# A hybrid DeltaNet and attention block: decayed keys in zero-padded tiles of 128 rows, and other orders around them

## The chip, the cores and the metric

One core of a Trainium2 chip. The metric is the device time of one execution in microseconds (us); lower is better. The products run on TensorE (PE), sums and differences on VectorE (DVE), copies, scalings and exponentials on ScalarE (ACT), a part of the differences on GpSimd (POOL), and the DMAs are issued by SyncE (SP).

## What is computed

One layer on 1024 positions of 1024 channels, in float32: a norm, an input projection, four heads of gated DeltaNet and eight heads of banded attention on it, a gated mix of both, an output projection, a second norm, an up projection with a causal convolution and a gate, a down projection, and a last norm. Of the reference, the part that the change is about, over 16 chunks of 64 positions:

```python
kd_c = k * jnp.exp(G[..., -1:] - G)[..., None]        # the decayed keys, 64 x 128 a chunk
gl_c = gam[..., -1]

def step(s, xs):
    w_i, uv_i, p_i, qg_i, kd_i, gl_i = xs
    u = uv_i - jnp.einsum('bhid,bhde->bhie', w_i, s)
    o = jnp.einsum('bhid,bhde->bhie', qg_i, s) + jnp.einsum('bhij,bhje->bhie', p_i, u)
    s = gl_i[..., None, None] * s + jnp.einsum('bhid,bhie->bhde', kd_i, u)
    return s, o
```

and the outer frame:

```python
mix = jax.nn.sigmoid(ga) * (oa @ w_branch_a[l]) + jax.nn.sigmoid(gb) * (ob @ w_branch_b[l])
x = x + mix @ w_out[l]
h = rmsnorm(x, norm_ffn_w[l])
u = causal_dwconv(h @ w_up[l], conv_ffn_w[l]) + conv_ffn_b[l]
gate, up = jnp.split(u, 2, axis=-1)
x = x + (jax.nn.silu(gate) * up) @ w_down[l]
```

## The kernel before

The large projections are products of 128x128 with 128x512. Each float32 operand is split into a high part (a cast by ScalarE) and a low part (the difference, by VectorE or GpSimd), and each product is three: high with low, high with high, low with high (BH and BL are the normed input, whi and wlo a weight, psph the result). They take some 0.23 us each on TensorE. The products inside the DeltaNet are float32 as they are; each is two instructions in the trace (x2).

The program's stages on the chip's clock: norm and first projections to about 60 us; four DeltaNet heads to about 475; attention in four pairs of heads to 746; the mix of both branches to 850; output projection and norm to 940; the up stage to 1365; the down stage to 1578; the last norm.

**DeltaNet.** The loop over h runs from -1 to 3. Stage h issues the chain of head h and prepares head h + 1, with fillers between: projections and convolutions of head h + 2, gate halves (`gates`, 24 products each, of which stage h takes `GFILL[h + 1]`), and z. `gdn_prep` transposes the keys on TensorE into PSUM (psk) and makes nKs (a copy) and Kd (scaled by the decay) from there, both on ScalarE. `gdn_prep2` transposes the values, makes the decays by two exponentials (decb, decT) and then scales nKs and Vs, 128x128 at a time. A triangular solve follows. The tables `APP`, `APK` and `QN` say after how many fillers the solve is applied (`gdn_apply`, which opens U) and the queries' norm is taken (`gdn_qnorm`).

`gdn_chain` does 16 chunks, two (e = 0 and 1) to each p. Each chunk: the product psws of WQ (queries and solved keys, 128 rows) with the state S; VectorE adds it to U (64 rows) and puts its other half in O; the product pss of Kd with U over the chunk's 64 rows; VectorE makes the next S from S and pss. After two chunks comes pso.

An order of the instructions is found by a scheduler from priorities; `behind()` issues what follows after a named instruction (the last product, or the last of another kind that was noted in `last`).

**End of attention.** The last attention pair is woven with what is left of `gates`, then come the projections of the branches (oh and ol of the DeltaNet's output, bh and bl of attention's).

**Up stage.** A Strassen-like form with seven products P1 to P7 for a pair of blocks, with sums in PSUM on VectorE between them. At its start (line 1333 on) the last operands are made from the second norm's transposes, and the first pair of blocks is begun. From here on the order on each engine is the order of the code (`V`, `S`, `G`, `Q` and the first product of each group are pinned).

**Down stage.** The same form: `plan` is P1, P5, P6, P3, P7, P2, P4, eleven steps each, of 12 products. `prep_w` makes, two steps at a time, the sums W of weights (VectorE), their high parts (wdh, ScalarE) and low parts (wdl, VectorE), two steps ahead for the sums.

Of the kernel before, what the change touches and what calls it, by code (L numbers as in the profile page):

```python
# [16 lines left out]
P = 128  # L17
# [18 lines left out]
APP = (10, 10, 10, 2)  # L36
APK = (7, 4, 3, None)
QN = (7, 3, 4, 5)
PR0 = 1
GFILL = (4, 4, 5, 5, 4)  # L40
# [6 lines left out]
def hybrid_kernel(ctx: ExitStack, tc: tile.TileContext, a):  # L47
# [176 lines left out]
    def first_rms(e):  # L224
# [3 lines left out]
        for i in range(4):  # L228
            xt = gp.tile([P, D], F32, tag=("Kd", "U")[i % 2], name="xt", bufs=2)
# [38 lines left out]
    wraw, whi, wlo = (gw.tile([P, KT, P], dt, tag=tg, name="wv") for dt, tg in ((F32, "sq"), (F32R, "nKs"), (F32R, "Vs")))  # L268
# [89 lines left out]

    def bc3(ap, n):

        return ap.unsqueeze(2).broadcast_to([P, NT, n])
# [38 lines left out]
    def gdn_prep(c):  # L400
# [13 lines left out]
        Kd = gp.tile([P, NT, P], F32, tag="Kd", name="Kd", bufs=2)  # L414
# [8 lines left out]
        for e in range(2):  # L423
# [6 lines left out]
            for i in range(4):  # L430
                nc.scalar.activation(Kd[:, 4 * e + i, :], pks[e][:, i, :], AF.Copy, scale=eg[:, 2, 4 * e + i, h:h + 1])
            for i in range(4):
                nc.scalar.activation(jk, nKs[:, 4 * e + i, :], AF.Square, accum_out=ssk[:, 4 * e + i:4 * e + i + 1])
        nc.vector.tensor_scalar_add(ssk, ssk, EPS)
# [6 lines left out]
    def gdn_prep2(c):  # L441
# [19 lines left out]
        nc.scalar.activation(decT.rearrange("p n j -> p (n j)"), psd2, AF.Exp)  # L461
# [24 lines left out]
        for p in range(NT):  # L486
            nc.scalar.activation(nKs[:, p, :], nKs[:, p, :], AF.Copy, scale=nks[:, p:p + 1])
            nc.scalar.activation(Vs[:, p, :], Vs[:, p, :], AF.Copy, scale=bv[:, p:p + 1])
# [34 lines left out]
    def gdn_apply(c):  # L523
# [17 lines left out]
        U = gp.tile([P, NT, P], F32, tag="U", name="U", bufs=2)  # L541
# [14 lines left out]
    def gdn_chain(c):  # L556
# [6 lines left out]
        for p in range(NT):  # L563
            for e in range(2):
# [7 lines left out]
                mm(ps2, Kd[r, p, :], U[r, p, :], start=True, stop=True)  # L572
# [22 lines left out]
    def gdn_qnorm(c):  # L595

        sqq = gw.tile([P, NT, P], F32, tag="sq", name="sqq")
        nc.scalar.activation(sqq, c["WQ"][:, :, 64:192], AF.Square)
        psn = psc.tile([P, 8], F32, tag="c", name="psn")
        for p in range(NT):  # L600
            side.append(lambda p=p: mm(psn[:, p:p + 1], sqq[:, p, :], ones, start=True, stop=True))
        c["psn"] = psn
# [741 lines left out]
    prs[1].P2(True)  # L1344
    sub(BL[:, k1, s], b22, BH.bitcast(F32)[:, k1, s])
# [25 lines left out]
    p, r = prs  # L1371
    p.P5()
    p.sum_q()
    p.sum_pa()
    r.sum_pa()
    p.P6()
    p.sum_pc()
# [93 lines left out]
    def prep_w(k):  # L1471

        n = min(2, NS - 2 * k)
        for s in range(2 * k + 2, min(2 * k + 4, NS)):
            w_sum(s)
# [325 lines left out]
```

## Time and profile before

| | us |
|---|---|
| median of 3 runs | 1591.93 (1590.27 to 1592.96) |
| the profiled execution's own time | 1592.53 |
| its span in the trace | 1590.6 |
| TensorE busy | 1542.7 (97%) |
| VectorE busy | 1120.3 (70%) |
| ScalarE busy | 698.0 (44%) |
| GpSimd busy | 595.6 (37%) |

The span goes from the first instruction of the trace to the last; the time is a little longer. Busy time of TensorE is that in which a product is in work, not that in which it runs at its peak: the ends of products are modelled, products overlap, and only the distance from start to start tells what one costs. The granted clock is 1.00 at 2.4 GHz and 0.5 at 1.2 GHz; its mean over the span is 0.994.

### The profile page before, as it was taken

What the parts mean: (1) busy time and instruction counts of PE and PEld (TensorE: products, weight loads), DVE (VectorE), ACT (ScalarE), POOL (GpSimd) and SP (SyncE); (2) the same over time, 40 slices, a digit from 0 to 9 for tenths busy, and PEclk for the clock granted to TensorE, in tenths of its full rate; (3) what the DMA queues carried; (4) which work ended last, traced back from release to release, by engine and by line L of the source; (5) the groups of instructions that cost most, each with busy time, mean ns of one, the idle gap of its engine ahead of it and who ended that gap; (6) DMA issues with size and microseconds to landing.
All of it is one profiled execution on the core that took longest, in us unless ns stands there. A gap on an engine that the chain in (4) does not pass through costs nothing.

```text
span 1590.6 us, 21158 instructions
## 1 busy us (share of the span) xinstructions
PE 1542.7 (97%) x7687; PEld 1255.8 (79%) x7687; DVE 1120.3 (70%) x2150; ACT 698.0 (44%) x1376; POOL 595.6 (37%) x449
## 2 busy tenths in 40 slices
PE   8999999999999999999999999999999999999997
PEld 6777776877777787888887887888888888788885
DVE  6795867948436878875665566777777777787787
ACT  7535334352225655654222244444444444433344
POOL 2422212212131101110220148877777776233353
PEclk9999999999999999999999999999999999999998
DMA  7021121122131101122654222233332332775533
GB/s 294 27 73 59 56 73 38 46 77 68 60 123 48 32 26 44 36 73 81 194 167 139 90 80 86 90 114 111 115 108 100 100 100 74 246 245 172 177 93 139
DMA packets 74504, 162.03 MB, mean 102 GB/s; under 512 B 15648, under 2 KB 16928, under 8 KB 74400
## 3 DMA queue, kind: packets, MB, share of 16 engines
q1 hardware_dynamic: 74400, 160.68, 30.5%
q8 instruction: 60, 0.98, 0.3%
q14 instruction: 44, 0.36, 0.1%
HBM read 120.55 MB, written 40.11 MB: 101 GB/s over the span
## 4 chain that ended last, share of the span: by engine, by line
PE 49%; DVE 3%; DMA 2%; ACT 1%; issue 1%; SPq 0%; POOL 0%; POOLq 0%; DVEq 0%; ACTq 0%
PE psph L52 8%; PE pb L52 7%; PE psd L52 7%; PE psout L52 5%; PE pc L52 5%; PE pa L52 4%; PE pb L1141 4%; PE psd L1493 3%; PE pc L1141 2%; PE pa L1141 2%; DMA araw<-dA 1%; DVE yu L1155 1%; PE pso L52 0%; DMA oaT<-dO 0%; DVE wdl L1155 0%
## 5 line engine op out<-in xcount | busy, mean ns | idle before, releaser
L82 POOL TENSOR_TENSOR wlo<-wraw,whi 128x1024 fp32r<-128x1024 f32 (+1 forms) x57 | 120.2, 2108 | 464.7 <-ACT whi L81 259.5
L52 PE MATMUL psph<-BH,whi 128*128 128x512 f32 x688 | 280.4, 408 | 10.1 <-ACT BH L220 5.2
L52 PE MATMUL psph<-BH,wlo 128*128 128x512 f32 x688 | 275.9, 401 | 1.7 <-POOL wlo L82 1.7
L52 PE MATMUL psph<-BL,whi 128*128 128x512 f32 x688 | 277.4, 403 | 0.0
L52 PEld LDWEIGHTS psph<-BH,whi 128*128 128x128 f32 x688 | 130.8, 190 | 34.8 <-ACT BH L220 5.9
L1155 POOL TENSOR_TENSOR ol<-wraw,oh 128x512 fp32r<-128x512 f32 x110 | 150.6, 1386 | 9.1 <-ACT oh L1155 9.1
L52 PEld LDWEIGHTS psph<-BH,wlo 128*128 128x128 f32 x688 | 130.8, 190 | 26.0 <-POOL wlo L82 2.1
L52 PEld LDWEIGHTS psph<-BL,whi 128*128 128x128 f32 x688 | 130.7, 190 | 23.1 <-DVE BL L221 1.0
L52 PE MATMUL psd<-wdl,ah 128*128 128x512 f32 (+1 forms) x311 | 121.6, 391 | 5.4 <-DVE wdl L1155 5.4
L1155 POOL TENSOR_TENSOR al<-araw,ah 128x1024 fp32r<-128x1024 f32 (+1 forms) x28 | 70.5, 2518 | 143.7 <-ACT ah L1155 143.6
L1155 POOL TENSOR_TENSOR wraw<-wraw 128x512 f32<-128x512 f32 x86 | 119.5, 1389 | 4.9
L1493 PE MATMUL psd<-wdh,al 128*128 128x512 f32 (+1 forms) x311 | 121.1, 390 | 0.0
L52 PE MATMUL psd<-wdh,ah 128*128 128x512 f32 (+1 forms) x311 | 119.8, 389 | 0.0
L1155 ACT CAST oh<-wraw 128x512 fp32r<-128x512 f32 x110 | 67.8, 621 | 102.0 <-POOL wraw L1155 101.9
L1155 DVE TENSOR_TENSOR wdl<-W,wdh 128x512 fp32r<-128x512 f32 x77 | 88.4, 1186 | 30.7 <-ACT wdh L1155 30.7
L1155 ACT CAST ah<-araw 128x1024 fp32r<-128x1024 f32 (+1 forms) x39 | 40.6, 1041 | 115.9 <-issue 48.8
L81 ACT CAST whi<-wraw 128x1024 fp32r<-128x1024 f32 (+2 forms) x61 | 55.4, 908 | 78.9 <-PE psph L52 55.1
L1155 POOL TENSOR_TENSOR gl<-wraw,gh 128x512 fp32r<-128x512 f32 x42 | 55.9, 1332 | 69.6 <-ACT gh L1155 69.6
L52 PEld LDWEIGHTS psd<-wdl,ah 128*128 128x128 f32 x311 | 58.8, 189 | 20.0 <-DVE wdl L1155 7.9
L1141 PE MATMUL pa<-BH,gh 128*128 128x512 f32 x176 | 68.6, 389 | 0.0
L52 PE MATMUL pa<-BH,gl 128*128 128x512 f32 x176 | 68.5, 389 | 0.0
L52 PE MATMUL pa<-BL,gh 128*128 128x512 f32 x176 | 68.5, 389 | 0.0
(342 smaller groups left out, 3826.2 us busy)
## 6 DMA issues: line engine op xcount, KB each, us to landing
wraw<-w_up SPq DMA_DIRECT2D x44, 512.0 KB, 4.9
wraw<-w_tiles SPq DMA_DIRECT2D x42, 512.0 KB, 3.5
araw<-dA SPq DMA_DIRECT2D x77, 256.0 KB, 3.0
dA<-yu SPq DMA_DIRECT2D x33, 512.0 KB, 3.1
W<-w_down SPq DMA_DIRECT2D x44, 256.0 KB, 4.7
xt<-x SPq DMA_DIRECT2D x16, 512.0 KB, 5.0
dG<-gt SPq DMA_DIRECT2D x16, 512.0 KB, 2.8
ta<-dG SPq DMA_DIRECT2D x16, 256.0 KB, 2.7
```

The lines of the kernel that those rows point to most:

```text
L52: last["mm"] = nc.tensor.matmul(*args, **kw).ins
L81: nc.scalar.copy(hi, src)
L82: (eng or nc.gpsimd).tensor_tensor(out=lo, in0=src, in1=hi.bitcast(F32), op=ALU.subtract)
L1141: i = nc.tensor.matmul(ps, wh[:, k], xh[:, k], start=start and k == 0, stop=False, **kw)
L1155: return lambda *args, **kw: tc.keep_in_program_order(f(*args, **kw))
L1493: i = nc.tensor.matmul(ps, al[:, j, ts], wh[:, es], start=False, stop=stop, **kw)
```

## The change

Six things at once.

1. Kd is no tile from a rotating buffer any more, but two permanent tiles `Kds`, one for even and one for odd heads, with 128 rows for each chunk. GpSimd clears both once. `gdn_prep2` fills the 64 rows of each chunk by ScalarE from nKs in SBUF, 16 copies of 64x128 a head, between the scalings of nKs and Vs and behind the exponential decT. The product pss then runs over 128 rows of Kd and U.
2. Buffers: the loads of x share three buffers (they had four), the third weight of the start uses the room of kf, U has one buffer instead of two, sqq that of zs.
3. The addition to ssk goes from VectorE to GpSimd.
4. Tables: the first stage takes 6 gate halves instead of 4, so two fewer remain for the end of attention; `APP`, `APK` and `QN` shift the solve's application and the queries' norm.
5. At the start of the up stage P5, q, P6 and pc of the first pair are written ahead of the last operands.
6. In the down stage the sums W for P4 (W21 - W12, written over W12, which no later product needs) are made during P2's steps, eleven steps sooner.

```diff
--- before.py
+++ after.py
@@ -33,11 +33,11 @@
 C2 = (0, 3, 3, 1)
 C3 = (0, 4, 4, 4)
 OUT = (0, 3, 5, 3, 8)
-APP = (10, 10, 10, 2)
-APK = (7, 4, 3, None)
-QN = (7, 3, 4, 5)
+APP = (11, 10, 10, 2)
+APK = (2, 4, 3, None)
+QN = (7, 5, 7, 5)
 PR0 = 1
-GFILL = (4, 4, 5, 5, 4)
+GFILL = (6, 4, 5, 5, 4)
 PRI = 4000
 AHEAD = 2
 BAND = 640
@@ -226,7 +226,8 @@
         s = slice(e * HN, (e + 1) * HN)
         psr = psa.tile([P, HN], F32, tag="a", name="psrb")
         for i in range(4):
-            xt = gp.tile([P, D], F32, tag=("Kd", "U")[i % 2], name="xt", bufs=2)
+            pool, tag = ((gp, "U"), (gp, "Lr"), (gw, "vf"))[i % 3]
+            xt = pool.tile([P, D], F32, tag=tag, name="xt")
             nc.sync.dma_start(xt, a["x"][(4 * e + i) * P:(4 * e + i + 1) * P, :])
             ssq = sml.tile([P, 1], F32, tag="ssq", name="ssq")
             nc.scalar.activation(xt, xt, AF.Square, accum_out=ssq)
@@ -265,7 +266,7 @@
     nea = prm[:, 61:65]
     nc.scalar.activation(nea, nea, AF.Exp)
     nc.vector.tensor_scalar_mul(nea, nea, -1.0)
-    wraw, whi, wlo = (gw.tile([P, KT, P], dt, tag=tg, name="wv") for dt, tg in ((F32, "sq"), (F32R, "nKs"), (F32R, "Vs")))
+    wraw, whi, wlo = (gw.tile([P, KT, P], dt, tag=tg, name="wv") for dt, tg in ((F32, "kf"), (F32R, "nKs"), (F32R, "Vs")))
     nc.sync.dma_start(wraw, a["w_tiles"][2 * GH])
     split(wraw, whi, wlo, nc.vector)
     ws.append((whi, wlo))
@@ -356,6 +357,12 @@
         nc.gpsimd.memset(t_, 0.0)
         zts.append(t_)
 
+    Kds = []
+    for i in range(2):
+        t_ = gp.tile([P, NT, 2, P], F32, name=f"Kd{i}")
+        nc.gpsimd.memset(t_, 0.0)
+        Kds.append(t_)
+
     def bc3(ap, n):
 
         return ap.unsqueeze(2).broadcast_to([P, NT, n])
@@ -411,7 +418,7 @@
             en.tensor_tensor(out=gl, in0=m_, in1=bc3(glo.bitcast(F32)[:, :, h], CH), op=ALU.mult)
             gms.append((gh.rearrange("p n j -> p (n j)"), gl.rearrange("p n j -> p (n j)")))
         nKs = gw.tile([P, NT, P], F32, tag="nKs", name="nKs")
-        Kd = gp.tile([P, NT, P], F32, tag="Kd", name="Kd", bufs=2)
+        Kd = Kds[h % 2]
         Vs = gw.tile([P, NT, P], F32, tag="Vs", name="Vs")
         ssk = gp.tile([P, NT], F32, tag="ssk", name="ssk", bufs=2)
         rk = gp.tile([P, NT], F32, tag="rk", name="rk", bufs=2)
@@ -428,10 +435,8 @@
             pks.append(psk.rearrange("p (n d) -> p n d", d=P))
             nc.scalar.copy(nKs[:, 4 * e:4 * e + 4, :], pks[e])
             for i in range(4):
-                nc.scalar.activation(Kd[:, 4 * e + i, :], pks[e][:, i, :], AF.Copy, scale=eg[:, 2, 4 * e + i, h:h + 1])
-            for i in range(4):
                 nc.scalar.activation(jk, nKs[:, 4 * e + i, :], AF.Square, accum_out=ssk[:, 4 * e + i:4 * e + i + 1])
-        nc.vector.tensor_scalar_add(ssk, ssk, EPS)
+        nc.gpsimd.tensor_scalar_add(ssk, ssk, EPS)
         rsqrt(rk, ssk)
         nc.gpsimd.tensor_mul(bv, beta[:, :, h], rk)
         nc.gpsimd.tensor_mul(nb, bv, rk)
@@ -458,7 +463,7 @@
         mm(psd2, mgtR, gms[1][0], start=True, stop=False)
         mm(psd2, mgtR, gms[1][1], start=False, stop=True)
         decT = gp.tile([P, NT, CH], F32, tag="decT", name="decT")
-        nc.scalar.activation(decT.rearrange("p n j -> p (n j)"), psd2, AF.Exp)
+        last["exp"] = nc.scalar.activation(decT.rearrange("p n j -> p (n j)"), psd2, AF.Exp).ins
         nc.vector.tensor_tensor(out=decT, in0=decT, in1=m64[1], op=ALU.mult)
 
         psG = psa.tile([P, HN], F32, tag="a", name="psG")
@@ -483,9 +488,14 @@
             for e in range(2):
                 mm(psQ[e * CH:(e + 1) * CH, p * CH:(p + 1) * CH], kf[:, p * P + e * CH:p * P + (e + 1) * CH],
                    WQ[:, p, 64 + e * CH:64 + (e + 1) * CH], start=True, stop=True)
-        for p in range(NT):
-            nc.scalar.activation(nKs[:, p, :], nKs[:, p, :], AF.Copy, scale=nks[:, p:p + 1])
-            nc.scalar.activation(Vs[:, p, :], Vs[:, p, :], AF.Copy, scale=bv[:, p:p + 1])
+        Kd = c["Kd"]
+        with behind("exp"):
+            for p in range(NT):
+                for e in range(2):
+                    r = slice(e * CH, (e + 1) * CH)
+                    nc.scalar.activation(Kd[r, p, e, :], nKs[r, p, :], AF.Copy, scale=eg[r, 2, p, h:h + 1])
+                nc.scalar.activation(nKs[:, p, :], nKs[:, p, :], AF.Copy, scale=nks[:, p:p + 1])
+                nc.scalar.activation(Vs[:, p, :], Vs[:, p, :], AF.Copy, scale=bv[:, p:p + 1])
         pt = ptA[h % 2]
         for e in range(2):
             r = slice(e * CH, (e + 1) * CH)
@@ -538,7 +548,7 @@
             nc.scalar.copy(zt[r0, :, r1], psx2[r0, 0:256].rearrange("p (n j) -> p n j", j=32))
 
         WQ, nKs, Vs = c["WQ"], c["nKs"], c["Vs"]
-        U = gp.tile([P, NT, P], F32, tag="U", name="U", bufs=2)
+        U = gp.tile([P, NT, P], F32, tag="U", name="U")
         for q in range(2):
             n = slice(4 * q, 4 * q + 4)
             psW = psa.tile([P, HN], F32, tag="a", name="psW")
@@ -569,7 +579,7 @@
                 nc.vector.tensor_add(U[r, p, :], ps[r], U[r, p, :])
                 nc.vector.tensor_scalar_mul(O[rx, p, :], ps[rx], eg[rx, 1, p, h:h + 1])
                 ps2 = psc.tile([P, P], F32, tag="c", name="pss")
-                mm(ps2, Kd[r, p, :], U[r, p, :], start=True, stop=True)
+                mm(ps2, Kd[:, p, e, :], U[:, p, :], start=True, stop=True)
                 S2 = gp.tile([P, P], F32, tag="S", name="S", bufs=3)
                 last["dve"] = nc.vector.scalar_tensor_tensor(out=S2, in0=S, scalar=eg[:, 3 + e, p, h:h + 1], in1=ps2,
                                                              op0=ALU.mult, op1=ALU.add).ins
@@ -594,7 +604,7 @@
 
     def gdn_qnorm(c):
 
-        sqq = gw.tile([P, NT, P], F32, tag="sq", name="sqq")
+        sqq = gp.tile([P, NT, P], F32, tag="zs", name="sqq")
         nc.scalar.activation(sqq, c["WQ"][:, :, 64:192], AF.Square)
         psn = psc.tile([P, 8], F32, tag="c", name="psn")
         for p in range(NT):
@@ -1342,6 +1352,11 @@
         next(steps1)
     prs[1].keep(S)
     prs[1].P2(True)
+    p, r = prs
+    p.P5()
+    p.sum_q()
+    p.P6()
+    p.sum_pc()
     sub(BL[:, k1, s], b22, BH.bitcast(F32)[:, k1, s])
     sub(hf[:, k1], hf[:, k1], tf[:, k1])
     vsplit(hf[:, k1], BH[:, k0, s], BL[:, k0, s])
@@ -1368,13 +1383,8 @@
         Q.dma_start(dA[5:7, i].rearrange("s p t -> p s t"), y1.rearrange("p (s t) -> p s t", s=2))
 
     ys = []
-    p, r = prs
-    p.P5()
-    p.sum_q()
     p.sum_pa()
     r.sum_pa()
-    p.P6()
-    p.sum_pc()
     p.gate_a()
     r.P5()
     r.sum_q()
@@ -1472,7 +1482,10 @@
 
         n = min(2, NS - 2 * k)
         for s in range(2 * k + 2, min(2 * k + 4, NS)):
-            w_sum(s)
+            if plan[s // FH][0] == "P2":
+                w_sum(s + FH)
+            elif plan[s // FH][0] != "P4":
+                w_sum(s)
         for s in range(2 * k, 2 * k + n):
             S.copy(whs[s % 5], w_block(s))
         for s in range(2 * k, 2 * k + n):
```

ScalarE's order in the preparation of the first head, behind the exponential decT. Before (nKs and Vs are the keys and values that are scaled):

```order
L461 ACTIVATE decT<-psd_758 128x512
L383 ACTIVATE th<-acc 128x512
L487 ACTIVATE nKs<-nKs,nks 128x128
L488 ACTIVATE Vs<-Vs,bv 128x128
L487 ACTIVATE nKs<-nKs,nks 128x128
L488 ACTIVATE Vs<-Vs,bv 128x128
L487 ACTIVATE nKs<-nKs,nks 128x128
L488 ACTIVATE Vs<-Vs,bv 128x128
```

The change (Kd filled from nKs, in two halves, with the same scalings between):

```order
L466 ACTIVATE decT<-psd_753 128x512
L496 ACTIVATE Kd_291<-nKs,eg 64x128 x2
L498 ACTIVATE Vs<-Vs,bv 128x128
L497 ACTIVATE nKs<-nKs,nks 128x128
L496 ACTIVATE Kd_291<-nKs,eg 64x128 x2
L498 ACTIVATE Vs<-Vs,bv 128x128
L497 ACTIVATE nKs<-nKs,nks 128x128
L496 ACTIVATE Kd_291<-nKs,eg 64x128 x2
```

Behind the exponential stand 32 instructions instead of 16; the copies to Kd from psk have left the place ahead of decb.

TensorE's order behind the last attention products (pso). Before, gate products of the normed input BH, BL:

```order
L52 MATMUL pso<-PTh_4256,V 128x256
L52 MATMUL pso<-PTl_4257,V 128x256
L52 MATMUL psph<-BH,wlo 128x512
L52 MATMUL psph<-BH,whi 128x512
L52 MATMUL psph<-BL,whi 128x512
L52 MATMUL psph<-BH,wlo 128x512
L52 MATMUL psph<-BH,whi 128x512
```

The change, with the branches' products (oh, ol, bh, bl):

```order
L52 MATMUL pso<-PTh_4350,V 128x256
L52 MATMUL pso<-PTl_4351,V 128x256
L52 MATMUL psph<-oh_6520,wlo 128x512
L52 MATMUL psph<-oh_6526,whi 128x512
L52 MATMUL psph<-ol_6527,whi 128x512
L52 MATMUL psph<-oh_6526,wlo 128x512
L52 MATMUL psph<-oh_7209,whi 128x512
L52 MATMUL psph<-bh_7215,whi 128x512
L52 MATMUL psph<-ol_7210,whi 128x512
L52 MATMUL psph<-oh_7209,wlo 128x512
L52 MATMUL psph<-bl_7219,whi 128x512
L52 MATMUL psph<-bh_7215,wlo 128x512
```

The 43 gate products between the last pso and the first product of a branch are gone from here.

VectorE's order at the start of the up stage, before (q and pc are sums of the first pair, XT3l, BL and hf operands, pa sums of both pairs):

```order
L1155 TENSOR_TENSOR XT3l<-tf,XT3h 128x4x128
L1155 TENSOR_TENSOR BL<-pst,BH 128x4x128
L1155 TENSOR_TENSOR hf<-hf,tf 128x512
L1155 TENSOR_TENSOR BL<-hf,BH 128x4x128
L1155 TENSOR_TENSOR q<-pc,p_8611 128x512
L1155 TENSOR_TENSOR pa<-pa,p_8611 128x512
L1155 TENSOR_TENSOR pa<-pa,p_8700 128x512
L1155 TENSOR_TENSOR pc<-pb,q 128x512
```

and with the change:

```order
L1165 TENSOR_TENSOR XT3l<-tf,XT3h 128x4x128
L1165 TENSOR_TENSOR q<-pc,p_8643 128x512
L1165 TENSOR_TENSOR pc<-pb,q 128x512
L1165 TENSOR_TENSOR BL<-pst,BH 128x4x128
L1165 TENSOR_TENSOR hf<-hf,tf 128x512
L1165 TENSOR_TENSOR BL<-hf,BH 128x4x128
L1165 TENSOR_TENSOR pa<-pa,p_8643 128x512
L1165 TENSOR_TENSOR pa<-pa,p_8732 128x512
```

q and pc have moved ahead of three operands and two sums.

## Rows read from the trace of the kernel before

**Rows 1.** The page's first lines: the span, and each engine's busy time, its share of the span and its instructions.

```profile
span 1590.6 us, 21158 instructions
...
PE 1542.7 (97%) x7687; PEld 1255.8 (79%) x7687; DVE 1120.3 (70%) x2150; ACT 698.0 (44%) x1376; POOL 595.6 (37%) x449
```

**Rows 2.** The table of stretches over the whole span, four of them: from and to, length, then busy time and instructions of each engine, TensorE's granted clock as a share of full speed, the DMA engines' mean share and GB/s.

```profile
163.00:182.00 19.00, 18.49 (x87) 13.42 (x86) 17.15 (x42) 4.90 (x11) 2.88 (x4) 1.00 0.17 56
...
252.00:283.00 31.00, 28.56 (x124) 20.57 (x124) 24.39 (x61) 7.32 (x19) 6.61 (x7) 0.94 0.18 56
...
335.00:358.00 23.00, 23.00 (x164) 16.94 (x164) 14.33 (x37) 14.11 (x53) 4.66 (x6) 1.00 0.11 30
358.00:382.00 24.00, 22.00 (x96) 15.59 (x96) 19.64 (x62) 5.07 (x14) 4.77 (x2) 0.93 0.21 67
```

**Rows 3.** The view of the tile Kd: operation, number, duration in ns (least, median, greatest), first and last start, shapes. The first is the product pss, the second the filling of Kd.

```profile
L52 PE MATMUL pss<-U,Kd x128: 272/373/579, 137.4 to 452.1; 64*128 64x128 f32 x128
L431 ACT ACTIVATE Kd<-psk,eg x32: 359/387/425, 66.8 to 338.4; 128x128 f32<-128x128 f32 x32
```

**Rows 4.** TensorE's timeline from 242.1 to 244.8: start, duration of one (of all together where x2), line, operation, tiles and shapes.

```profile
242.19 0.39 PE L52 MATMUL psph<-BH,whi 128*128 128x512 f32 x1
242.42 0.38 PE L52 MATMUL psws<-S,WQ 128*128 128x128 f32 x2
242.56 0.48 PE L52 MATMUL psph<-BL,whi 128*128 128x512 f32 x1
242.88 0.40 PE L52 MATMUL psph<-BH,wlo 128*128 128x512 f32 x1
243.11 0.40 PE L52 MATMUL psph<-BH,whi 128*128 128x512 f32 x1
243.44 0.48 PE L52 MATMUL pss<-U,Kd 64*128 64x128 f32 x2
243.85 0.50 PE L52 MATMUL psph<-BL,whi 128*128 128x512 f32 x1
244.19 0.39 PE L52 MATMUL psph<-BH,wlo 128*128 128x512 f32 x1
...
244.66 0.39 PE L52 MATMUL psws<-S,WQ 128*128 128x128 f32 x2
```

**Rows 5.** VectorE's timeline of the same stretch; in brackets the time that the engine stood idle ahead of an instruction, and what ended it.

```profile
242.37 0.16 DVE L434 TENSOR_SCALAR ssk<-ssk 128x8 f32<-128x8 f32 x1
242.84 0.28 DVE L569 TENSOR_TENSOR U<-psws,U 64x128 f32<-64x128 f32 x1 [0.32 <-PE psws L52]
...
243.96 0.35 DVE L574 SCALAR_TENSOR_TENSOR S<-S,eg,pss 128x128 f32<-128x128 f32 x1 [0.44 <-PE pss L52]
```

**Rows 6.** VectorE's and TensorE's timelines about 172.5: U and the pss behind it.

```profile
172.43 0.27 DVE L569 TENSOR_TENSOR U<-psws,U 64x128 f32<-64x128 f32 x1
...
172.76 0.49 PE L52 MATMUL pss<-U,Kd 64*128 64x128 f32 x2 [0.51 <-DVE U L569]
```

**Rows 7.** The table of stretches for the instructions on tile Kd alone (x is their number).

```profile
163.00:182.00 19.00, 3.40 (x14) 2.06 (x14) 0.00 (x0) 1.00 0.17 56
...
252.00:283.00 31.00, 4.61 (x19) 2.75 (x18) 0.00 (x0) 0.94 0.18 56
...
358.00:382.00 24.00, 4.19 (x16) 2.56 (x16) 0.00 (x0) 0.93 0.21 67
```

**Rows 8.** The view of line 487, the scaling of nKs on ScalarE: number, duration in ns (least, median, greatest), first and last start.

```profile
L487 ACT ACTIVATE nKs<-nKs,nks x32: 386/391/407, 76.9 to 349.1; 128x128 f32<-128x128 f32 x32
```

**Rows 9.** The start of the up stage: VectorE's timeline (q and pc), TensorE's, and one stretch behind them in the table of stretches.

```profile
959.74 0.68 DVE L1155 TENSOR_TENSOR q<-pc,p 128x512 f32<-128x512 f32 x1
...
961.53 0.68 DVE L1155 TENSOR_TENSOR pc<-pb,q 128x512 f32<-128x512 f32 x1
...
962.27 0.50 PE L1141 MATMUL pb<-XT3h,oh 128*128 128x512 f32 x1 [2.11 <-DVE pc L1155]
...
963.70:967.10 3.40, 3.40 (x9) 2.67 (x9) 1.07 (x2) 0.00 (x0) 3.40 (x3) 0.51 0.85 287
```

**Rows 10.** The end of attention: the timelines of TensorE (the first product behind the last attention product), ScalarE (bh) and VectorE (bl).

```profile
746.77 0.40 PE L52 MATMUL psph<-BH,wlo 128*128 128x512 f32 x1
...
747.36 3.91 ACT L81 CAST bh<-obT 128x1024 fp32r<-128x1024 f32 x4
...
748.52 3.50 DVE L82 TENSOR_TENSOR bl<-obT,bh 128x1024 fp32r<-128x1024 f32 x3 [0.72 <-ACT bh L81]
```

**Rows 11.** The end of the down stage: what TensorE waits for from 1535 to 1575 (total us, times, longest), VectorE's W ahead of wdl, GpSimd's al, the stretch behind them, and VectorE's wdl in P2's steps.

```profile
PE psd L52 <- DVE wdl L1155: 3.9, 3, 2.5
...
1563.37 3.48 DVE L1155 TENSOR_TENSOR W<-W,W 128x512 f32<-128x512 f32 x2
...
1562.74 2.96 POOL L1155 TENSOR_TENSOR al<-araw,ah 128x1024 fp32r<-128x1024 f32 x1
...
1567.90:1571.30 3.40, 3.40 (x10) 2.66 (x9) 2.96 (x5) 2.08 (x3) 1.52 (x1) 0.50 0.34 139
...
1526.21 3.07 DVE L1155 TENSOR_TENSOR wdl<-W,wdh 128x512 fp32r<-128x512 f32 x2 [0.61 <-ACT wdh L1155]
```

**Rows 12.** The start: ScalarE's cast of the tile wv, and the products with it in the view of that tile.

```profile
19.78 1.05 ACT L81 CAST wv<-wv 128x1024 fp32r<-128x1024 f32 x1
...
L52 PE MATMUL psph<-BH,wv x32: 388/389/393, 24.4 to 51.1; 128*128 128x512 f32 x32
```

## The prediction

> **What bounds the kernel now.** I read the page's head first. TensorE is busy for 1542.7 of 1590.6 us (97%); VectorE, ScalarE and GpSimd stand at 70, 44 and 37% [rows 1]. So time comes from two places only: what TensorE's own products take, and the some 48 us in which it waits. The table of stretches then says where the change lands. The four chains of the DeltaNet lie in stretches where TensorE is busy nearly throughout, but with two kinds of cover: in three of them VectorE is busy for 17.15 of 19, 24.39 of 31 and 19.64 of 24 us, elsewhere for less (14.33 of 23) [rows 2]. A busy TensorE is not one at its peak, so I looked at the products one by one. That is where the main term is.
>
> The profiled execution took 1592.53 us (span 1590.6); the sum is made against it. The median shown is 1591.93, 0.6 less, which comes off at the end. A measurement of this kernel can tell about 0.2% (3.2 us) from no change.
>
> **A. The product with the decayed keys.** Every chunk has two fp32 products of 128x128, two instructions each: WQ with S (psws, all 128 rows) and Kd with U (pss, 64 rows now, 128 after the change with half of them zeros). There are 128 pss instructions, 64 pairs [rows 3]. The timeline of TensorE shows both kinds among the same filler products [rows 4]:
> - psws: 242.19 (filler), 242.42 (the pair), 242.56, 242.88: 0.69 us from the start of the filler before to the second one behind.
> - pss: 243.11, 243.44, 243.85, 244.19: 1.08 us.
>
> The difference is 0.39 us a pair. It is no wait for data: U ends at 242.84 + 0.28 = 243.12 and pss starts at 243.44, 0.32 later [rows 4, 5], while at a place where pss did wait for U (172.43 + 0.27 = 172.70) it started at 172.76, 0.06 after it [rows 6]. So the 0.1 us ahead of the pair, the 0.27 inside and the 0.02 behind belong to the 64 rows. With 128 rows I expect the spacing of psws: 64 x 0.39 = 25.0 us is the most that can come back.
>
> Not all will, since a faster TensorE meets the loop S, psws, U, pss, S. After U (243.12) pss would still start some 0.2 later: covered. S starts at 243.96 and ends at 244.31 [rows 5], and the next psws starts at 244.66 [rows 4], 0.30 after the 0.05 that a result needs; TensorE would take 0.29 out of this distance. So a quiet pair keeps all its gain with about nothing to spare, and a pair behind a long VectorE instruction doesn't. The three VectorE-heavy stretches hold 14 + 19 + 16 pss instructions [rows 7], 24 pairs; I let them keep half: 40 x 0.39 + 24 x 0.195 = **-20.3 us**. Bounds: nothing in the 24 pairs, -15.6; everything, -25.0.
>
> **The new fill of Kd.** 8 ScalarE copies of 128x128 from PSUM a head, 0.39 us each [rows 3], become 16 of 64x128 behind the exponential. As each costs between nothing and 0.39, ScalarE gets 0 to 3.2 us more a head. ScalarE is busy 44% [rows 1] and what follows (nKs, Vs scaled, nKs at 0.39 each [rows 8]) feeds the solve of the next head, which fillers cover: **0**, bounds -2 to +2 (gone are copies that hold a PSUM buffer, added are 16 instructions ahead of the solve). If the cover were gone it would be 4 x 3.2 = 13. The two clears and the ssk addition go to GpSimd (37%) with the same answer.
>
> **B. The start of the up stage.** TensorE waits 2.11 us at 962.27 for VectorE's pc, which stands at 961.53 behind q (959.74) and two pa sums [rows 9]; and 1.4 us later the granted clock is 0.51 for 3.4 us [rows 9], that is 1.2 instead of 2.4 GHz, behind the wait in which TensorE stood still. Half of 3.4 is lost: 1.7. With the change q and pc stand ahead of three operand instructions and the pa sums. pc then needs P6 alone, which lies well ahead of P7's end. What is late next are those operands, needed only by later products. Taken **-3.5**; bounds 0 (another instruction becomes as late) and -3.8.
>
> **C. The end of attention.** Two gate halves move forward to the first stage. Before, 43 gate products followed the last attention product (from 746.77 on [rows 10]; 43 x 0.23, the spacing of fillers from 242.19 to 242.42 [rows 4], is 9.9 us), and under them ScalarE split ob (bh, 4 in 3.91 us from 747.36) and VectorE made bl (3 in 3.50 from 748.52) [rows 10]. That cover goes: in the new order five oh products are followed by bh and bl, 19 products with the last of them. Unhindered they are through at 746.77 + 19 x 0.23 = 751.1. But VectorE has ol and four bl, 1.14 apart, from about 748.5: the last ends at 748.52 + 4 x 1.14 + 1.2 = 754.3, TensorE's half column at about 754.8. **+3.7**; bounds 0 and +5.4 (with one stretch at 1.2 GHz, 1.7 as in B). The products themselves are only moved: the first stage gets 48 and gives them back here.
>
> **D. The end of the down stage.** Between 1535 and 1575 TensorE waits 3.9 us in three stalls for wdl, the longest 2.5 [rows 11]. There VectorE makes W (2 in 3.48 us, slowed beside al on GpSimd, 2.96 from 1562.74) ahead of wdl [rows 11]; the clock is 0.50 for 3.4 us behind it, another 1.7 [rows 11]. The change makes these W sums during P2's steps. Two W of 0.68 or so leave each step: 1.36 of the 2.5, and most of the smaller two, up to all 3.9 and the 1.7: -5.6. In P2's steps the sums stand ahead of wdl (1526.21, 3.07 for two, with 0.61 idle ahead [rows 11]); 1.36 more than fills that idle time, so up to +1.5 there, +1 if nothing else is gained. Taken **-3.0**, bounds -5.6 to +1.
>
> **E. Start.** The x loads get three buffers instead of four: the fourth waits for ScalarE's square of the first. The loads are bound by the queue, and the first product with wv comes at 24.4, after its cast at 19.78 [rows 12]. About 1 us of play: **0**, bounds 0 to +1.5.
>
> **Sum.** -20.3 - 3.5 + 3.7 - 3.0 + 0 = -23.1; 1592.53 - 23.1 = 1569.4, as a median 1568.8: **1569**.
>
> **The rivals.**
> 1. VectorE's loop decides in every pair (R2). For: the play after S is about nothing, and short strays such as the 0.16 us ssk instruction ahead of U [rows 5] stand between its links. Against: in the quiet stretches VectorE idles before both U and S [rows 5]. If the 24 heavy pairs keep nothing and the 40 others 0.39 - 0.16 = 0.23, A is -9.2 and the sum -12: **1580**.
> 2. Loads decide inside the pair (R3). If the pair's own time (0.41, 243.44 to 243.85 [rows 4]) comes from loading each matrix only after the product before, the 128 rows keep it and only 0.12 comes back: 40 x 0.12 + 24 x 0.06 = 6.2, sum -9.0: **1583**. Against it: the 128-row psws pair takes 0.14 (242.42 to 242.56 [rows 4]). The Trainium skill ("TensorE: Matmul & The Clock Gate", Part 3, "The mechanism") has it that a weight load overlaps products in flight only where the row group differs; by that a 64-row load would be the better placed one and a padded one would gain nothing inside the pair. The rows of psws, which has all row groups and is spaced closest, disagree.
> 3. The 0.39 has nothing to do with the rows (R4): U as a freshly written operand, say. Then A is 0 and the sum -2.8: about **1589**. Against: U was ready 0.32 before.
> 4. Slower (R5): ScalarE's burst of 32 instructions behind the exponential (32 x 0.29 = 9.4 us, the mean of 0.39 and half of it for the 64-row ones) stands in front of the U copies that open the next head's chain. With no cover at all this is 4 x 9.4 = 37.6 against a gain of 23.1: **about 1606**. It decides from 6 us a head on. Against: 16 such instructions stand there now, and in the stretch with the last of them (last start of nKs 349.1 [rows 8]) TensorE is busy for all of its 23 us [rows 2].
>
> **How the numbers follow.** Chances: forecast 0.66, R2 0.18, R3 0.05, R4 0.06, R5 0.05. The forecast's own range is 1559 to 1578 (A between its bounds, B, C and D not all at one end). To hold 8 in 10 the whole reaches up to R2 and R3: 1559 to 1583; R4 and R5 are left out with the outer tails. Only R5 is slower: 0.05; R4 stands at the limit of 0.2%, half of its chance is no change: 0.03; the rest is faster: 0.92.
>
> **What would show it.** A right: 128-row pss pairs with the spacing of psws (about 0.14 to the next product), and TensorE's waits for U and S in the heavy stretches no more than doubled. Wrong: spacing of 0.41 kept, or a wait for U or S at most pairs. B: no wait for pc, no half clock behind 963. C: a new wait for bl near 750. D: less wait for wdl from 1540 on, and perhaps some from 1512. The burst: waits of TensorE for ScalarE's U, nKs or WQ copies near the start of each chain; these would make the whole prediction wrong.

## Result, and the profile after

The changed kernel takes 1572.84 us (median, 1570.79 to 1573.51), the kernel before 1592.33 beside it: ratio 0.9878, 95% interval [0.9861, 0.9895], 19.5 us less. A second measurement later gave 0.9894 [0.9879, 0.9908]. The forecast was 1569 in a range of 1559 to 1583, 23.1 us less. The profiled execution took 1573.51, with a span of 1571.7. The head of its page answers to [rows 1]:

```profile
span 1571.7 us, 21185 instructions
...
PE 1520.5 (97%) x7687; PEld 1246.0 (79%) x7687; DVE 1122.3 (71%) x2146; ACT 715.4 (46%) x1408; POOL 597.3 (38%) x455
```

TensorE's busy time fell by 22.2 us at the same number of instructions (7687). The starts of landmark products on TensorE, in us, show where the time went (the last column is the change within the stage that ends there):

| landmark | before | after | shift | in the stage |
|---|---|---|---|---|
| first product with wv | 24.45 | 25.65 | +1.20 | +1.2 |
| last product of attention | 746.65 | 737.59 | -9.06 | -10.3 |
| last product with oh, near the end of the branches | 841.38 | 824.71 | -16.67 | -7.6 |
| first product of the up stage | 939.43 | 922.73 | -16.70 | 0.0 |
| first product of the down stage | 1361.14 | 1340.99 | -20.15 | -3.4 |
| last instruction | 1590.59 | 1571.72 | -18.87 | +1.3 |

48 products of 0.227 us more lie ahead of attention's end now (43 of the gates and 5 with oh): 10.9 us of work moved out of the stage of the third row into that of the second. So the heads and attention became 21.2 us shorter, the end of attention 3.3 longer, the up stage 3.4 shorter, and the down stage 1.3 longer where 3.0 less had been forecast.

**The pairs.** TensorE's timeline of a pss and a psws among fillers answers to [rows 4], and VectorE's U and S beside it to [rows 5]:

```profile
246.75 0.40 PE L52 MATMUL psph<-BH,whi 128*128 128x512 f32 x1
246.99 0.38 PE L52 MATMUL pss<-U,Kd 128*128 128x128 f32 x2
247.12 0.48 PE L52 MATMUL psph<-BL,whi 128*128 128x512 f32 x1
247.44 0.39 PE L52 MATMUL psph<-BH,wlo 128*128 128x512 f32 x1
247.67 0.40 PE L52 MATMUL psph<-BH,whi 128*128 128x512 f32 x1
247.90 0.40 PE L52 MATMUL psws<-S,WQ 128*128 128x128 f32 x2
248.05 0.48 PE L52 MATMUL psph<-BL,whi 128*128 128x512 f32 x1
...
246.49 0.28 DVE L579 TENSOR_TENSOR U<-psws,U 64x128 f32<-64x128 f32 x1 [0.38 <-PE psws L52]
...
247.41 0.35 DVE L584 SCALAR_TENSOR_TENSOR S<-S,eg,pss 128x128 f32<-128x128 f32 x1 [0.25 <-PE pss L52]
```

From the filler ahead of pss (246.75) to the second product behind (247.44) it is 0.69 us, where it was 1.08. pss starts 0.22 after U has ended (246.77), as worked out. S ends at 247.76 and psws follows at 247.90, 0.14 later, where it was 0.35.

Why the rows matter is seen in the weight loads (TensorE's loads, PEld, after and then before):

```profile
246.82 0.36 PEld L52 LDWEIGHTS pss<-U,Kd 128*128 128x128 f32 x2
247.10 0.19 PEld L52 LDWEIGHTS psph<-BL,whi 128*128 128x128 f32 x1
...
243.44 0.29 PEld L52 LDWEIGHTS pss<-U,Kd 64*128 64x128 f32 x2 [0.37 <-DVE U L569]
243.85 0.19 PEld L52 LDWEIGHTS psph<-BL,whi 128*128 128x128 f32 x1
```

After, Kd's load starts at 246.82 and its product at 246.99; the load of the filler behind starts at 247.10, ahead of its product at 247.12. Before, Kd's load and its product both stood at 243.44, and the next load stood at 243.85 with its product [rows 4]: neither the 64-row load nor the 128-row load behind it was made ahead of time. Over all 64 pairs the first load of Kd starts 0.15 us ahead of its product (median), where it was 0.00. So by these rows the 0.39 us are loads that did not lie behind a running product; why a 64-row load is not made ahead, no run shows. The Trainium skill ("TensorE: Matmul & The Clock Gate", Part 3, "The mechanism") says that a load overlaps products in flight only where the row group differs. These rows are against it: loads of all 128 rows overlap products of all 128 rows, and the load of 64 of them didn't. The same section of the Trainium skill also lets a load be pulled ahead into a background weight buffer. Loads of 128 rows do start ahead here, but no row shows which buffer a load goes to.

The loads also show where the reserve behind S went. The load for psws, after and then before:

```profile
247.81 0.30 PEld L52 LDWEIGHTS psws<-S,WQ 128*128 128x128 f32 x2 [0.18 <-DVE S L584]
...
244.43 0.42 PEld L52 LDWEIGHTS psws<-S,WQ 128*128 128x128 f32 x2
```

What it loads is WQ, the operand that the kernel names first, not S, and still it starts 0.05 us after S has ended (247.76). It does so in 55 of the 64 pairs, before in 7; the load of Kd starts 0.05 after U's end in 59, before in 6. The reserve is used up. The products lose little by it: the median psws pair takes 0.02 us more.

The view of the tile Kd, as in [rows 3]:

```profile
L52 PE MATMUL pss<-U,Kd x128: 270/274/378, 140.9 to 443.2; 128*128 128x128 f32 x128
L496 ACT ACTIVATE Kd<-nKs,eg x64: 384/394/400, 73.1 to 353.1; 64x128 f32<-64x128 f32 x64
```

A copy of 64 rows costs ScalarE as much as one of 128, 0.39 us: the fill took the upper bound, 3.2 us more a head, and nobody waited for it.

**What TensorE waits for.** From 60 to 240, then at the end of attention (736 to 850), then in P2 and P4 (1496 to 1563):

```profile
PE psph L52 <- DVE gt L171: 3.1, 3, 1.8
PE psdec L52 <- issue: 1.4, 1, 1.4
PE psph L52 <- DVE u L381: 1.0, 1, 1.0
PE pss L52 <- DVE U L579: 0.9, 1, 0.9
...
PE psph L52 <- DVE bl L82: 0.9, 4, 0.4
PE psph L52 <- ACT oh L81: 0.6, 1, 0.6
...
PE psph L52 <- ACT bh L81: 0.4, 1, 0.4
...
PE psd L52 <- DVE wdl L1165: 3.4, 3, 1.7
PE psd L52 <- ACT wdh L1165: 1.5, 1, 1.5
```

The wait for pc at the start of the up stage is gone, those for bl, bh and oh are new, and the waits of the down stage are 4.9 us in all where they were 3.9 [rows 11].

### The profile page after: what moved, and what is told of

Same layout as the page of the kernel before. It is cut to its first block, busy times and chain, and to the rows that moved or that the text cites. A ratio compares the mean times of both kernels' runs of the same rounds, so it can differ in the third digit from the quotient of the medians.

```text
span 1571.7 us, 21185 instructions
## 1 busy us (share of the span) xinstructions
PE 1520.5 (97%) x7687; PEld 1246.0 (79%) x7687; DVE 1122.3 (71%) x2146; ACT 715.4 (46%) x1408; POOL 597.3 (38%) x455
## 4 chain that ended last, share of the span: by engine, by line
PE 49%; DVE 3%; issue 2%; DMA 1%; ACT 1%; SPq 1%; POOL 0%; POOLq 0%; DVEq 0%; ACTq 0%
PE psph L52 8%; PE pb L52 7%; PE psd L52 6%; PE psout L52 5%; PE pa L52 5%; PE pc L52 5%; PE pb L1151 4%; PE psd L1506 3%; PE pa L1151 2%; PE pc L1151 2%; DVE wdl L1165 1%; DVE yu L1165 1%; PE pso L52 1%; SPq L1165 1%; DMA araw<-dA 1%
## 5 line engine op out<-in xcount | busy, mean ns | idle before, releaser
L52 PEld LDWEIGHTS psd<-wdh,ah 128*128 128x128 f32 x311 | 58.8, 189 | 14.1 <-ACT wdh L1165 1.9
```

Of the source, the lines that this page charges most:

```text
L52: last["mm"] = nc.tensor.matmul(*args, **kw).ins
```

## The experiments

Ratios are to the kernel before, measured beside them; the changed kernel stands at 0.9878 and, measured again, 0.9894. A sum over the pairs is the time from the start of the product before a pair to that of the second behind it, over all 64 pairs, waits included. A stage's length is from its first product to the next stage's, that of P4 to its 133rd product (its last step comes in halves).

### Only the rows undone

```diff
-                mm(ps2, Kd[:, p, e, :], U[:, p, :], start=True, stop=True)
+                mm(ps2, Kd[r, p, e, :], U[r, p, :], start=True, stop=True)
```

> The changed kernel, but the product pss runs over the chunk's 64 rows again (the padded tiles, their fill and all other parts of the change stay). Theory (the rows set the distance of the products around pss): in the changed kernel's trace the 64 pss pairs with the product before and the two behind sum to 49.8 us, before to 69.9, while the psws pairs grew from 46.1 to 49.3; both go back, so 16.9 us are lost and the time is about 1572.8 + 16.9 = 1589.7, with 0.41 us from pss to the next product instead of 0.14. Up to 3.4 more if the two stretches at 1.2 GHz come back that the chains had before. Rival (the gain is due to the new order, the new fill or the buffers and not to the rows): 1573, whatever pss's distances.

Measured: 1587.93 us, ratio 0.9987 [0.9978, 0.9996]. The pss pairs sum to 68.7 us (49.8 in the changed kernel), the psws pairs to 45.5 (49.3): 15.1 us together. Its timeline has the old distance, 0.42 from pss to the next product, with the new tiles, fill and order all there:

```profile
249.42 0.40 PE L52 MATMUL psph<-BL,whi 128*128 128x512 f32 x1
249.74 0.48 PE L52 MATMUL pss<-U,Kd 64*128 64x128 f32 x2
250.16 0.49 PE L52 MATMUL pso<-U,ptA 128*128 128x128 f32 x2
```

This one line is worth 14.8 to 17.3 us (0.9987 less 0.9894 or 0.9878, of 1590): the rows carry nearly nine tenths of the gain (16.9 to 19.4).

### The padded keys alone

The kernel before with the tiles `Kds`, their fill and product, the buffers, ssk and QN; the other tables, the up stage and the sums as before:

```diff
-APP = (11, 10, 10, 2)
-APK = (2, 4, 3, None)
-GFILL = (6, 4, 5, 5, 4)
+APP = (10, 10, 10, 2)
+APK = (7, 4, 3, None)
+GFILL = (4, 4, 5, 5, 4)
-            if plan[s // FH][0] == "P2":
-                w_sum(s + FH)
-            elif plan[s // FH][0] != "P4":
-                w_sum(s)
+            w_sum(s)
...
```

> The kernel before with the padded tiles alone (their fill behind the exponential, the product over 128 rows, the buffers, ssk on GpSimd and the table QN, which the buffers need); gate halves, the solve's table, the up stage and the down stage's sums as before. Theory: 16.9 us come back in the pairs, 1.2 are lost at the start to the third buffer of x, and 0 to 3.4 come from stretches at 1.2 GHz that don't occur: 1592.3 - 16.9 + 1.2 = 1576.6, down to 1573. Rival (the two gate halves, moved to the first stage, are what makes the heads faster, as cover for waits): 1590 or more.

Measured: 1578.77, ratio 0.9930 [0.9915, 0.9945], 11.1 us below the kernel before, which is between the theory and its rival. The pairs give 13.1 us (pss 52.0 for 69.9, psws 51.0 for 46.1), and four stretches at 1.2 GHz lie ahead of 200 us (near 62, 76, 151 and 188). Waits stand there that the first profile of the changed kernel doesn't have, or has shorter (60 to 240 us):

```profile
PE pss L52 <- DVE U L579: 3.2, 2, 1.9
PE psd L52 <- DVE gil L418: 1.8, 1, 1.8
PE psoT L644 <- ACT O L636: 1.5, 1, 1.5
...
PE psB L52 <- DMA zt<-dZ: 0.8, 1, 0.8
```

To the changed kernel it is 5.7 to 8.3 us (0.9930 less 0.9894 or 0.9878, of 1590). The two profiles are 5.6 us apart. From the first product with wv to the first of the up stage this one is 6.8 us longer, and in the up stage 1.8; the start is 1.6 and the down stage 1.5 shorter. The 6.8 are the most that the tables can have here. The next run finds 1.8 of them in the gate halves. But the wait for gil and the stretches near 62 and 76 belong to the execution: the profile of "al on VectorE" below has them too, and there each engine's order in the heads is that of the changed kernel, and heads and attention take 2.9 us longer than in its first profile. What of the rest is the earlier solve (`APK`) and what the other two stretches at 1.2 GHz (1.7 each) stays open.

In the up stage this profile has the old wait of 2.1 us for pc (until 950.82), but no half clock behind it:

```profile
951.00:957.00 6.00, 6.00 (x27) 4.96 (x28) 3.96 (x6) 2.81 (x5) 5.76 (x5) 1.00 0.63 186
```

### The gate halves back

```diff
-APP = (11, 10, 10, 2)
+APP = (10, 10, 10, 2)
-GFILL = (6, 4, 5, 5, 4)
+GFILL = (4, 4, 5, 5, 4)
```

> The changed kernel with the two gate halves back at the end of attention (and the first stage's solve applied one filler sooner, as the shorter list of fillers needs). The prediction's step C (moving them gave nothing ahead of the attention and cost 3.7 behind it): about 3.5 us faster than the changed kernel. Rival, from the runs so far (padded keys alone came to 0.993 of before and the whole change to 0.988, 8 us more, of which the up stage is 3.5 and the down stage -1.3): the halves cover waits in the first stage, and these come back with up to three stretches at 1.2 GHz of 1.7 each: 4 to 6 us slower than the changed kernel. Then the wait for bl after the attention is gone and waits for gil, U or O ahead of 190 us are there.

Measured: 1574.77, ratio 0.9906 [0.9889, 0.9922], against 1572.96 for the changed kernel measured beside it: 1.8 slower, with intervals that overlap, so less than the rival expected and not the gain of step C. The trace shows both sides. From the last attention product to the last with oh it is 94.3 us (before 94.7; the changed kernel 87.1 and the 10.9 moved, 98.0): no wait for bl, 3.7 us better. But in the first stage (60 to 240), and the stretch behind it:

```profile
PE psB L52 <- DMA zt<-dZ: 2.8, 1, 2.8
...
131.00:137.80 6.80, 6.80 (x60) 5.63 (x57) 0.00 (x0) 1.09 (x3) 0.00 (x0) 0.50 0.23 80
```

The solve's trip through DRAM has no cover any more, TensorE waits 2.8 us for it (until 129.22), and the clock of 0.50 for 6.8 us behind costs 3.4. The moved halves cover a wait here and uncover one there.

### The changed kernel once more

> The changed kernel as it is, beside the next three on the same chip. 0.9878 of the kernel before, as first measured; its profile shows in which places the granted clock falls to 0.5 from one execution to the next.

Measured: 1572.96, 0.9894. The first product with wv came at 24.65 (25.65 in the first profile, 24.09 to 27.12 in the other runs with three buffers): the start differs from execution to execution by more than the 1.2 us in the table above. The clock fell near 1555 (1556 in the first profile) and at the very end, and nowhere in the heads.

### The start of the up stage undone

```diff
-    p, r = prs
-    p.P5()
-    p.sum_q()
-    p.P6()
-    p.sum_pc()
     sub(BL[:, k1, s], b22, BH.bitcast(F32)[:, k1, s])
...
     ys = []
+    p, r = prs
+    p.P5()
+    p.sum_q()
     p.sum_pa()
     r.sum_pa()
+    p.P6()
+    p.sum_pc()
```

> The changed kernel with the start of the up stage in its old order. Theory B: the wait of 2.1 us for pc comes back, and with it the stretch at 1.2 GHz (1.7): 1572.8 + 3.5 = 1576.3. Rival (the 3.5 us came from a stretch at 1.2 GHz that the shifted stages before would have avoided anyway): 1572.8 + 0 to 2, with the wait but with the granted clock at 1.00.

Measured: 1575.84, ratio 0.9910 [0.9896, 0.9923], 2.5 to 5.1 us slower than the changed kernel. The up stage takes 421.7 us, as before, against 418.3. The wait is back, and so is the half clock behind it (944 to 950 at 0.72, 1.7 us lost), although everything ahead of it had shifted by 17 us:

```profile
PE pb L1151 <- DVE pc L1165: 2.1, 1, 2.1
...
944.00:950.00 6.00, 5.12 (x15) 4.09 (x16) 3.29 (x6) 1.47 (x3) 5.76 (x5) 0.72 0.56 175
```

The wait comes with the order, in each of the three profiles that have it. The half clock doesn't always: with the padded keys alone it was absent, and the up stage took 420.1.

### The sums back

```diff
-            if plan[s // FH][0] == "P2":
-                w_sum(s + FH)
-            elif plan[s // FH][0] != "P4":
-                w_sum(s)
+            w_sum(s)
```

> The changed kernel with the sums W for P4 made two steps ahead, as before. The prediction's step D (the sums stood in the way of wdl at the end): 1572.8 + 3.0 = 1575.8. The rival that the two traces suggest (P2's steps lost 0.9 us and P4's 0.5 by the move, and the stall at the end belongs to GpSimd's al, beside which any VectorE instruction takes 2.9 us): 1572.8 - 1.3 = 1571.5, with P2 in 31.1 us and P4 in 34.1 instead of 32.0 and 34.6.

Measured: 1571.61, ratio 0.9884 [0.9871, 0.9898]: the times don't tell it from the changed kernel, but the stages do. P2 takes 31.1 us (32.0 in the changed kernel) and P4 34.15 (34.6), as forecast by the rival. Moving the sums cost 1.4 us; it saved nothing.

### al on VectorE

```diff
-        (V if k % 2 and plan[2 * k // FH][0] in ("P5", "P6", "P7", "P4") else G).tensor_tensor(
+        (V if plan[2 * k // FH][0] == "P4" or k % 2 and plan[2 * k // FH][0] in ("P5", "P6", "P7") else G).tensor_tensor(
```

> The changed kernel with every al of P4 made by VectorE, where now every other one is GpSimd's. Theory (the stall at the end of the down stage comes from GpSimd's al, beside which the VectorE instruction that starts then, W before and wdl now, takes 2.9 us instead of 0.7): the wait for wdl of 0.86 goes, al itself costs VectorE 1.2, P4 becomes 0.9 us shorter or more; the 1.5 us wait for the last ah stays, since that waits for a DMA. Rival (VectorE is simply full there): P4 gets longer by the 1.2 us of each added al, 2 to 3 us in all.

Measured: 1568.81, ratio 0.9867 [0.9853, 0.9882], 4.2 below the changed kernel measured beside it. P4 takes 29.7 us instead of 34.7. First VectorE and GpSimd in the changed kernel, then VectorE at the same place of this one:

```profile
1541.56 1.29 DVE L1165 SCALAR_TENSOR_TENSOR ot<-x,rsf,wn 128x1024 f32<-128x1024 f32 x1 [0.38 <-POOL rsf L1165]
1542.77 3.48 DVE L1165 TENSOR_TENSOR wdl<-W,wdh 128x512 fp32r<-128x512 f32 x2
...
1542.13 2.96 POOL L1165 TENSOR_TENSOR al<-araw,ah 128x1024 fp32r<-128x1024 f32 x1
...
1541.48 1.28 DVE L1165 SCALAR_TENSOR_TENSOR ot<-x,rsf,wn 128x1024 f32<-128x1024 f32 x1 [0.38 <-POOL rsf L1165]
1542.68 1.22 DVE L1165 TENSOR_TENSOR al<-araw,ah 128x1024 fp32r<-128x1024 f32 x1
1543.81 1.29 DVE L1165 TENSOR_TENSOR wdl<-W,wdh 128x512 fp32r<-128x512 f32 x2
```

Two wdl take 3.48 us beside GpSimd's al, just as the two W did at this place before [rows 11], and 1.29 without it. With al of 1.22 on its own queue VectorE is through at 1545.1 instead of 1546.25. The expectation was too small (0.9) and held the 1.5 us wait for the last ah to stay: it fell to 0.4, and the half clock behind it (1.7 us) is gone too.

### al on VectorE, sums back, operand loads ahead of the output's

```diff
+            w_sum(s)
...
+        (V if plan[2 * k // FH][0] == "P4" or k % 2 and plan[2 * k // FH][0] in ("P5", "P6", "P7") else G).tensor_tensor(
...
-        if k > 2 and 2 * (k + 2) < NS:
-            a_load(k + 2)
         while loads and loads[0][0] <= s + 1:
...
         if s + 4 == NS - 1:
             prep(k + 2)
+        if 2 * (k + 3) < NS:
+            a_load(k + 3)
```

> The changed kernel with the sums W for P4 made two steps ahead as before, every al of P4 on VectorE, and each load of the down stage's operand issued ahead of the output's DMAs that wait for the norm, instead of behind them. Theory: P2 takes 31.1 us instead of 32.0; in P4 the wait behind GpSimd's al and the 1.5 us for the last ah go, 34.6 becomes 31.5 to 32.5 (29.9 is a stage with no wait, 1.7 less where no stretch at 1.2 GHz follows a wait): 3 to 4 us faster than the changed kernel. Rival (the sums are too much for VectorE beside al): P4 stays above 34.

Measured: 1568.82, ratio 0.9868 [0.9853, 0.9882]. P2 31.1 and P4 31.3, beside 32.0 and 29.7 in the run before: the sums put back give 0.9 in P2 and cost 1.6 in P4 once al is on VectorE. So if the earlier loads do nothing, the move of the sums pays 0.7 there, which the times don't show; of the loads themselves no gain is seen.

### al of P2 as well

```diff
-        (V if k % 2 and plan[2 * k // FH][0] in ("P5", "P6", "P7", "P4") else G).tensor_tensor(
+        (V if plan[2 * k // FH][0] in ("P2", "P4") or k % 2 and plan[2 * k // FH][0] in ("P5", "P6", "P7") else G).tensor_tensor(
```

> The changed kernel with every al of P2 and of P4 on VectorE (the sums W for P4 stay in P2's steps). Theory (the stalls for wdl in both stages come from GpSimd's al, beside which a VectorE instruction takes up to 2.9 us): P2 from 32.0 to about 30.5, P4 29.7 as in the run with P4's al alone, the whole 1.5 us below that run: 0.986 of the kernel before. Rival (P2's VectorE is full: evacuations, the sums W, wdl and now al): P2 stays at 32 or grows, the whole as in that run (0.9867) or slower.

Measured: 1566.72, ratio 0.9847 [0.9832, 0.9862], the fastest version: 24 us below the kernel before and 5 to 7.5 below the changed one. P2 takes 30.3 us and P4 29.5. Of the waits for wdl nothing is left between 1494 and 1562:

```profile
PE psd L52 <- ACT wdh L1165: 0.2, 1, 0.2
```

### O on ScalarE

```diff
-                nc.vector.tensor_scalar_mul(O[rx, p, :], ps[rx], eg[rx, 1, p, h:h + 1])
+                nc.scalar.activation(O[rx, p, :], ps[rx], AF.Copy, scale=eg[rx, 1, p, h:h + 1])
```

> The changed kernel with the other half of psws, O, scaled by ScalarE instead of VectorE (64 instructions of 0.36 us less in VectorE's queue, between U and S of each chunk). Theory (what the 128 rows save, 20.1 us in the pss pairs, is partly given back because the loop of U and S on VectorE now comes just in time: psws pairs 49.3 us instead of 46.1, TensorE's waits for U and S 9.2 instead of 5.9): the psws pairs fall towards 46 and the waits for U and S to 6 or less, the heads become 3 to 6 us shorter. Rival (the loop isn't limited by VectorE's queue but by its own latency, S to psws to U to pss to S): waits for U and S stay at about 9, no change within 1 us, or slower where ScalarE's queue delays O ahead of pso's addition.

Measured: 1579.11, ratio 0.9927 [0.9913, 0.9941], slower than the changed kernel. The waits up to 480 us:

```profile
...
PE pss L52 <- DVE U L579: 3.7, 3, 1.6
PE psws L52 <- DVE S L584: 3.1, 3, 1.7
PE pss L52 <- ACT O L580: 3.0, 2, 1.8
...
PE psB L52 <- DMA zt<-dZ: 1.5, 1, 1.5
```

U and S cost 6.8 us instead of 9.2, but pss waits 3.0 for O, and the psws pairs grow from 49.3 to 50.8 us. Two stretches at 1.2 GHz (near 258 and 357, 1.7 each) lie in the heads; heads and attention take 3.7 us longer than in the first profile of the changed kernel. So the loop is not freed by taking this work off VectorE. The scheduler's order changed with it (a wait for zt appears), so whether latency alone sets the loop stays open.

## Why the prediction was right, and where it was wrong

**A, the rows: the mechanism right, the size too large.** The distance fell from 1.08 to 0.69 in quiet pairs as worked out, and undoing that line alone takes 14.8 to 17.3 us back. The pss pairs gave 20.1 of the possible 25.0 us. What was underrated is the other product: a quiet pair was to keep "all its gain with about nothing to spare", yet the psws pairs grew by 3.2 us (0.685 to 0.707 in the median quiet pair, the rest as waits for S). TensorE's idle time for U in the heads grew from 4.5 to 7.3 us, that for S from 1.4 to 1.9; these lie in the pairs' sums, as do waits too short to show as idle. So -16.9 in the trace (-13.1 with the old tables), instead of -20.3. R2 had the loop decide in every pair. The loads do wait for S and U in nearly every pair, but the products follow 0.05 us behind S in 15 pairs only (3 before) and behind U in 10 (6 before), so R2's price was not paid.

**What filled the gap** had no term. In the heads before, TensorE waited 0.9 us for Kd, 1.7 for wlo and 0.7 for gih, and two stretches at 1.2 GHz cost 1.7 each; in the changed kernel's profiles none of these is there. The half clock is not even in the same place for one order of instructions. Seven profiles have the changed kernel's order in the heads, on every engine: both of its own, and those of the runs with the sums back, the up stage undone, and al on VectorE (three). Two stretches at 1.2 GHz lie ahead of 475 us in two of them (near 55 and 116, and near 62 and 76), one in a third (57), none in the other four; heads and attention are 18.2 to 21.7 us shorter than before. So what of the 3.4 us belongs to the change stays open.

**The fill: right.** Twice as many instructions at 0.39 us, the upper bound of 3.2 us a head, all hidden; R5 did not occur.

**B: right.** -3.4 in the up stage (-3.5 forecast), and undoing it alone restores wait and half clock. The wait is its sure part: with the padded keys alone, where the order is the old one, the clock stayed at 1.00 and the up stage took 1.8 us more than in the changed kernel.

**C: right for the stretch behind attention, incomplete ahead of it.** +3.3 for +3.7. But "The products themselves are only moved" left out what they cover where they go: 2.8 us of a wait for zt and 3.4 us of half clock. In sum the move gains about nothing to 2 us, where step C had it cost 3.7.

**D: wrong, in size and sign.** +1.3 for -3.0, and outside the bound of +1. The step that failed is "1.36 of the 2.5, and most of the smaller two": it took W as the cause of the late wdl. The row of the sum said otherwise: two W took 3.48 us because GpSimd's al ran beside them. With W gone, wdl slid into the same 2.96 us and took 3.48 itself. P2 then paid 0.9 for the sums, also beside al. The stall that was left ended on a DMA (the last ah, 1.5 us), and the half clock followed it. ScalarE's last ah, TensorE's product behind it, and the clock:

```profile
1552.88 0.62 ACT L1165 CAST ah<-araw 128x512 fp32r<-128x512 f32 x1 [3.48 <-DMA araw<-dA]
...
1554.06 0.50 PE L52 MATMUL psd<-wdh,ah 128*128 128x512 f32 x1 [1.49 <-ACT wdh L1165]
...
1556.00:1560.00 4.00, 4.00 (x12) 3.15 (x11) 0.85 (x2) 0.72 (x2) 0.00 (x0) 0.57 0.00 0
```

Before, TensorE didn't wait there; the half clock ahead of that place (1567.90 to 1571.30 [rows 11]) may have hidden it, which no run tests. The runs with al on VectorE show the cause: 34.7 to 29.7, of which 1.7 is the half clock. It followed the last stall in five of the six profiles with the changed down stage; with the up stage undone the same waits stand there (3.4 and 1.5), the clock stayed at 1.00, and P4 was 1.6 us shorter.

**E: within its bounds.** +1.2 in one profile, +0.2 in the next; it varies as much from one execution to the next.

Against the forecast of -23.1 the first trace has -18.9 (the second -20.1). The miss of 4.2 us is D (4.3), E (1.2) and A (3.4), less 4.3 by which the heads became shorter than their pairs (21.2 for 16.9) and 0.4 from C.

## What to carry to other kernels

A product with a contraction over half the rows, placed among products of all rows, cost 0.39 us a pair more here than one padded with zeros; look at the starts of the weight loads, and try padding where memory allows. When a fast engine's instruction takes several times its usual time, ask which engine ran beside it before moving it: another instruction may take its place, as wdl took that of W. Filler work that is moved is priced at both ends, by what it covers there and what it uncovers here. A stretch at half clock is no sure price of an order: count it in several executions before giving it to a change.

## What the runs showed of the hardware

- A load of 64 rows among loads of 128 (or of 128 behind one of 64) started with its own product, not 0.02 to 0.17 us ahead of it; price 0.39 us for an fp32 pair.
- The weight load for psws, which reads WQ, started 0.05 us after the product's other operand, S, was made in 55 of 64 pairs of the changed kernel, and never sooner.
- A VectorE subtraction of 128x512 takes 0.68 us alone; two took 3.48 instead of 1.29 while GpSimd subtracted 128x1024 (2.96): the first of them lasted almost as long as the other engine's instruction.
- A ScalarE copy of 64x128 took 0.39 us, as one of 128x128.
- The same order of instructions met no, one or two stretches at 1.2 GHz in its heads from one execution to the next.
